# Triangular inverses one direction at a time, and 64-row products from compact operands

## The chip, the cores and the metric

The kernel runs on one core of a Trainium2 chip. The metric is the device time of one execution in microseconds (us). The engines are TensorE (PE; PEld is its loading of stationary operands), VectorE (DVE), ScalarE (ACT), GpSimd (POOL) and SyncE (SP), whose queue issues most of the DMAs.

## The reference, cut to what matters

Two residual blocks over 512 latent tokens (`S`) and 256 context tokens (`C`). The first has an attention layer and an "odd" layer with neighbourhood attention and a two-directional RWKV-7 scan; the second has a Mamba-2 scan and a gated delta rule (GDN), both in two directions, and a feed-forward network. RWKV and GDN run first over the context, and the state that comes out starts the run over the latent tokens. GDN in chunks of 64 tokens needs the solution of a unit triangular system per chunk, head and direction:

```python
a_mat = jnp.einsum("bclhd,bcshd->bclsh", k, k) * beta[:, :, :, None] * masked_exp(diff, strict)
lhs = jnp.moveaxis(a_mat, -1, 2) + jnp.eye(CHUNK, dtype=a_mat.dtype)
rhs = jnp.concatenate([v * beta[..., None], k * (beta * jnp.exp(g))[..., None]], -1)
sol = lax.linalg.triangular_solve(lhs, jnp.moveaxis(rhs, 3, 2), left_side=True, lower=True, unit_diagonal=True)
```

The RWKV recurrence `S = S*w - (S kk)(kk*a)^T + v k^T` is written in chunks in the same manner, so that it too needs the inverse of one unit triangular 64 x 64 matrix per chunk, head and direction. Products are float32; the large projections are split into a high and a low part (three products each).

## The kernel before, in words

All code is unrolled Python on a tile framework. The framework orders the instructions of each engine when the kernel is built: what is traced earlier has priority, and an instruction whose inputs are not ready lets later ones pass. After that the order is fixed. The program interleaves stages by generators: every `yield` gives the turn to the other generators, so the number of yields says how much of one stage is traced beside another. PSUM has 8 banks; pools take them by `bufs`, and a pool opened later waits for each bank until its last user is done.

The order around the change. `layer1` (L1331): **phase 1** of the RWKV context stream `c` (`rw_phase1`, L842), beside it `na_proj`; then phase 1 of the latent stream `l` with, as `self.side`, `rw_tri` and `rw_phase2` of the context stream (L1371 to L1374; one side step per iteration, two on odd iterations after the 16th); then `na_attn` (neighbourhood attention, L1205) with `rw_tri` of the latent stream stepped beside it (L1379 to L1382); then `rw_phase2` of the latent stream; then the output projection and the feed-forward network `f1`, whose side work is the whole context half of the second block, `ssm_ctx` (L2065), with its own triangular solve inside `ssm_tri`. `layer2` runs the latent half: `gdn_head`, then `ssm_tri` with `ssd_pair` ("pairs") and `gates` stepped beside it (L2157 to L2162), then the recurrence `gdn_rec` with `ssd_rec` and the output work.

`rw_dir` (L948) runs for each of 4 head pairs j and 2 directions d. It writes `az` (L983 to L989), a tile with zeros in one half of the partitions for each of the two heads, stores it (`dAf`, `dR`), multiplies it by `BKn` (L1004, 128 rows and both heads in one product), masks the result into `M` (L1006, DVE), multiplies `M` by `vu` (L1011), and copies (L1012, ACT). Groups of 2 chunks (latent) or 4 (context) share a PSUM bank.

`trisolve` (L769) inverts the 32 x 32 diagonal blocks of both directions by 31 steps of two DVE operations per direction: L792 multiplies into PSUM (`Tl`), L794 subtracts. The two directions alternate: multiply d0, multiply d1, subtract d0, subtract d1. There is a yield after every third step. Then ACT writes both transposes (L798) and the caller stores inverses and transposes of both directions (L1041: d0 on SP's queue, d1 on ACT's; L1735: all on SP's). There are four solves: RWKV context and latent, GDN context and latent. `rw_unit` (L1043) and `gdn_unit` (L1795) load them.

Of the kernel before, what the change touches and what calls it, by code (L numbers as in the profile page):

```python
# [766 lines left out]
class K1:  # L767

    def trisolve(self, pool, L, As, ps):  # L769


        nc = self.nc
        Zs, Ts = [], []
        for d in range(2):
            Z = pool.tile([128, 32, 32], F32, tag=f"Z{d}", name="Zl")
            nc.gpsimd.memset(Z, 0.0)
            nc.gpsimd.memset(Z.rearrange("p a b -> p (a b)")[:, ::33], 1.0)
            Zs.append(Z)
            Ts.append(ps[:, 256 * d:256 * d + 256])
        for n in range(1, 32):  # L780
            for op in range(2):
                for d in range(2):
                    A, Z = As[d], Zs[d]
                    if d == 0:
                        t = 32 - n
                        rows, cols, nr, ncl = slice(0, t), slice(t, 32), t, n
                    else:
                        t = n - 1
                        rows, cols, nr, ncl = slice(t + 1, 32), slice(0, t + 1), 31 - t, t + 1
                    tmp = Ts[d][:L, :nr * ncl].rearrange("p (a b) -> p a b", a=nr)  # L790
                    if op == 0:
                        nc.vector.tensor_tensor(tmp, A[:L, rows, t:t + 1].to_broadcast([L, nr, ncl]), Z[:L, t:t + 1, cols].to_broadcast([L, nr, ncl]), op=ALU.mult)  # L792
                    else:
                        nc.vector.tensor_tensor(Z[:L, rows, cols], Z[:L, rows, cols], tmp, op=ALU.subtract)  # L794
            if n % 3 == 0:
                yield
        for d in range(2):
            nc.scalar.activation(As[d][:L], Zs[d][:L].rearrange("p a b -> p b a"), AF.Copy)  # L798
        return Zs, As
# [42 lines left out]
    def rw_phase1(self, s):  # L842
# [4 lines left out]
        with ExitStack() as es:  # L847
# [7 lines left out]
            s.az = [pi.tile([128, s.nar, 2, n], F32, name=f"az{i}") for i in range(2)]  # L855
            s.vu = [pi.tile([128, s.nch, 128], F32, name=f"vu{i}") for i in range(2)]
            for z in s.az + s.vu:
                nc.gpsimd.memset(z, 0.0)
# [89 lines left out]
    def rw_dir(self, s, d, j, tp):  # L948
# [34 lines left out]
        for e in range(2):  # L983
            p = slice(64 * e, 64 * e + 64)
            if s.lat:
                nc.gpsimd.tensor_tensor(ch(az[p, 1, e]), ch(r[p]), E[p, :, i0:i0 + 64], op=ALU.mult)
                nc.sync.dma_start(s.dR[d][p, j], az[p, 1, e])
            nc.vector.tensor_tensor(ch(az[p, 0, e]), ch(kk[p]), E[p, :, iprev:iprev + 64], op=ALU.mult)
            nc.sync.dma_start(s.dAf[d][p, j], az[p, 0, e])  # L989
# [5 lines left out]
        w = nar * 128  # L995
        per = 512 // w
        mk = self.b(f"mar{d}")[:, :w].unsqueeze(1).to_broadcast([128, per, w])
        hc = max(per, nch // 2)
        for g in range(0, nch, per):
            if g % hc == 0:  # L1000
                M = tp.tile([128, hc, nar, 2, 64], F32, tag=f"M{d}", name="M", bufs=1)
            ps = s.psv("psA")
            for c in range(per):
                nc.tensor.matmul(ps[:, c * w:c * w + w], BKn[:, g + c].rearrange("p s t -> p (s t)"), az[:, :, :, (g + c) * 64:(g + c) * 64 + 64],  # L1004
                                 start=True, stop=True)
            nc.vector.tensor_tensor(M[:, g % hc:g % hc + per].rearrange("p c s e t -> p c (s e t)"), ps.rearrange("p (c x) -> p c x", c=per), mk, op=ALU.mult)  # L1006
            yield
            for c in range(g, g + per):
                for e in range(2):
                    o = ((c - g) // 2) * 128 + e * 64  # L1010
                    nc.tensor.matmul(ps[64 * (c % 2):64 * (c % 2) + 64, o:o + 64], M[:, c % hc, 0, e], vu[:, c, e * 64:e * 64 + 64], start=True, stop=True)  # L1011
            nc.scalar.activation(t2[:, g * 64:(g + per) * 64], ps[:, :per * 64], AF.Copy)  # L1012
            if (g + per) % hc == 0:
                g0 = g + per - hc
                for c in range(2):
                    nc.sync.dma_start(s.dA[d][:, c, g0 // 2:(g0 + hc) // 2, j].rearrange("p b e t -> p b (e t)"), M[0:64, c::2, 0].rearrange("p b e t -> p b (e t)"))
                if s.lat:
                    nc.sync.dma_start(s.dRR[d][:, j, g0:g0 + hc], M[:, :, 1].rearrange("p c e t -> p c (e t)"))
# [4 lines left out]
            yield  # L1023
        nc.sync.dma_start(s.dBV[d][:, j].rearrange("p b v -> p (b v)"), t2)

    def rw_tri(self, s):
        nc = self.nc
        Lq = 8 * s.nb
        with self.pool(name="tri", bufs=1, side="left") as trp, self.pool(name="trips", bufs=1, space=PSUM, side="right") as tps:
            As = [trp.tile([128, 32, 32], F32, tag=f"A{d}", name="Al") for d in range(2)]  # L1030
            for d in range(2):
                for p in range(4):
# [3 lines left out]
            Zs, ZTs = yield from self.trisolve(trp, 4 * Lq, As, tps.tile([128, 512], F32, name="Tl"))  # L1036
            for d in range(2):
                for z, dst in ((Zs[d], s.dZ[d]), (ZTs[d], s.dZT[d])):
# [364 lines left out]
class K2:  # L1403
# [308 lines left out]
    def ssm_tri(self, s):  # L1712
        nc = self.nc
        Lq = 8 * s.nb
        with self.pool(name="tri" + s.nm, bufs=1, side=s.side) as trp:
# [8 lines left out]
            else:  # L1724
                try:
                    while True:
                        next(tri)
# [384 lines left out]
    def layer2(self):  # L2112
# [20 lines left out]
        with ExitStack() as ps:  # L2133
# [23 lines left out]
            for _ in tri:  # L2157
                next(pairs, None)
                next(gates, None)
# [57 lines left out]
```

## Time and profile before

| | us |
|---|---|
| median of 3 runs | 3785.26 (3782.23 to 3792.06) |
| the profiled execution | 3793.68 |
| its span | 3791.9 |
| PE busy | 3377.0 |
| DVE busy | 1701.5 |

A row of a timeline has the start, the busy time, the engine, the line, the operation, the tiles (out<-in) and a count; in brackets stands how long the engine had been idle and what released it. A row by stretch has the length, the busy time of each engine with its number of instructions, the granted clock of PE (1.0 is 2.4 GHz, 0.5 is 1.2 GHz), and DMA. A row of waits has who waited for whom, us in total, times and the longest. The profiled execution is 0.2% above the median.

### The profile page before, as it was taken

To read this page: it belongs to the slowest core of one execution; us is meant where nothing else is said; L and a number is where in the kernel's file an instruction comes from. 1 tells how busy PE (TensorE), PEld (TensorE's weight loads), DVE (VectorE), ACT (ScalarE), POOL (GpSimd) and SP (SyncE) were. 2 spreads that over 40 slices of the span, in tenths; PEclk is the share of its full clock that TensorE was granted. 3 is DMA by queue.
4 is the path that set the end of the run, shared out by engine and by line. 5 is a ranking of instruction groups with operands and counts; after the bars stand their busy time and mean duration, and the time that the engine had idled before them with its cause. 6 is when DMAs were issued, how large, how long until landed. Compare 5 with 4: busy or idle time off the path is not lost. (4 is left out here: it accounts for less than half of the span.)

```text
span 3791.9 us, 49466 instructions
## 1 busy us (share of the span) xinstructions
PE 3377.0 (89%) x18772; PEld 2652.6 (70%) x18772; DVE 1701.5 (45%) x3170; ACT 1308.5 (35%) x2263; POOL 1402.0 (37%) x940
## 2 busy tenths in 40 slices
PE   7989989999999768888889989997898698789997
PEld 3679868787878546667768877666777457658885
DVE  4566231111124596574554426447657767431112
ACT  3366231121224433332234432333545323232222
POOL 1453222222223453321335544434544343244442
PEclk9999999999999878999889999998999899999999
DMA  6420243434334434636423433433455668512221
GB/s 230 164 106 7 88 151 117 150 116 141 126 106 129 111 111 140 175 88 204 146 70 124 131 105 95 122 93 99 140 155 155 158 193 247 164 61 95 95 97 65
DMA packets 397757, 480.78 MB, mean 127 GB/s; under 512 B 148432, under 2 KB 288656, under 8 KB 396496
## 3 DMA queue, kind: packets, MB, share of 16 engines
q1 hardware_dynamic: 384976, 476.05, 40.6%
q10 hardware_dynamic: 12544, 1.57, 0.3%
q8 instruction: 149, 2.44, 0.3%
q14 instruction: 88, 0.72, 0.1%
HBM read 391.86 MB, written 85.66 MB: 126 GB/s over the span
## 5 line engine op out<-in xcount | busy, mean ns | idle before, releaser
L322 POOL TENSOR_TENSOR wlo<-wraw,whi 128x1024 fp32r<-128x1024 f32 (+2 forms) x371 | 867.1, 2339 | 1512.7 <-ACT whi L321 1345.3
L321 ACT ACTIVATE whi<-wraw 128x1024 fp32r<-128x1024 f32 (+2 forms) x371 | 380.2, 1026 | 1041.3 <-issue 240.8
L504 DVE TENSOR_TENSOR pu<-pu,sg 128x512 f32<-128x512 f32 x88 | 55.6, 632 | 606.9 <-PE pu L361 554.2
L361 PE MATMUL pd<-hidh,wlo 128*128 128x512 f32 (+1 forms) x704 | 262.0, 372 | 9.2 <-POOL wlo L322 8.9
L361 PE MATMUL pd<-hidh,whi 128*128 128x512 f32 (+1 forms) x704 | 263.4, 374 | 6.1 <-ACT whi L321 3.8
L361 PE MATMUL pd<-hidl,whi 128*128 128x512 f32 (+1 forms) x704 | 260.5, 370 | 0.2 <-DVE hidl L506 0.2
L361 PE MATMUL pg<-hil,whi 128*128 128x512 f32 x528 | 214.3, 406 | 28.8 <-ACT hil L449 15.4
L361 PE MATMUL pg<-hil,wlo 128*128 128x512 f32 x528 | 211.4, 400 | 8.1 <-POOL wlo L322 7.1
L361 PE MATMUL pu<-hil,whi 128*128 128x512 f32 x528 | 209.7, 397 | 5.8 <-ACT whi L321 5.8
L361 PE MATMUL pu<-hil,wlo 128*128 128x512 f32 x528 | 209.2, 396 | 6.0 <-POOL wlo L322 6.0
L361 PE MATMUL pg<-lol,whi 128*128 128x512 f32 x528 | 210.5, 399 | 2.5 <-DVE lol L450 2.4
L361 PE MATMUL pu<-lol,whi 128*128 128x512 f32 x528 | 208.9, 396 | 0.0
L361 PE MATMUL psp<-hil,whi 128*128 128x512 f32 x416 | 174.0, 418 | 25.6 <-DVE yo L1782 11.8
L361 PE MATMUL psp<-lol,whi 128*128 128x512 f32 x416 | 171.0, 411 | 2.9 <-DVE lol L450 2.9
L361 PE MATMUL psp<-hil,wlo 128*128 128x512 f32 x416 | 170.3, 409 | 1.9 <-POOL wlo L322 1.8
L513 DVE SCALAR_TENSOR_TENSOR xT<-pd,mod,xT 128x512 f32<-128x512 f32 x80 | 59.8, 749 | 244.6 <-PE pd L361 244.6
L361 PEld LDWEIGHTS pd<-hidh,whi 128*128 128x128 f32 x704 | 133.3, 189 | 46.8 <-issue 15.1
L361 PEld LDWEIGHTS pd<-hidh,wlo 128*128 128x128 f32 x704 | 133.4, 189 | 39.1 <-POOL wlo L322 15.4
L361 PEld LDWEIGHTS pg<-hil,whi 128*128 128x128 f32 x528 | 101.5, 192 | 71.8 <-ACT hil L449 18.6
L361 PEld LDWEIGHTS pd<-hidl,whi 128*128 128x128 f32 x704 | 133.3, 189 | 24.0 <-issue 0.9
L792 DVE TENSOR_TENSOR Tl<-Al,Zl 64x31 f32<-64x31 f32 (+15 forms) x248 | 145.2, 585 | 4.1
L1574 DVE SCALAR_TENSOR_TENSOR psp<-xpl,vecs,psp 128x512 f32<-128x512 f32 x144 | 107.8, 751 | 84.5 <-ACT psp L1570 58.1
(588 smaller groups left out, 8145.9 us busy)
## 6 DMA issues: line engine op xcount, KB each, us to landing
mraw<-in_wm_dram SPq DMA_DIRECT2D x144, 512.0 KB, 4.3
wraw<-in_w2c_dram SPq DMA_DIRECT2D x72, 512.0 KB, 3.3
wraw<-in_wf0in_dram SPq DMA_DIRECT2D x44, 512.0 KB, 3.6
wraw<-in_wf1in_dram SPq DMA_DIRECT2D x44, 512.0 KB, 3.6
Z<-dZ SPq DMA_DIRECT2D x48, 256.0 KB, 3.8
ZT<-dZT SPq DMA_DIRECT2D x48, 256.0 KB, 4.1
wraw<-in_w1d_dram SPq DMA_DIRECT2D x23, 512.0 KB, 3.9
wraw<-in_wf2g_dram SPq DMA_DIRECT2D x22, 512.0 KB, 3.2
```

The costliest lines, as they stand in the source:

```text
L321: self.nc.scalar.activation(hi[:, :nk], t[:, :nk], AF.Copy)
L322: self.nc.gpsimd.tensor_tensor(lo[:, :nk], t[:, :nk], hi[:, :nk].bitcast(F32), op=ALU.subtract)
L361: nc.tensor.matmul(ps, l, r, start=first and i == 0 and p == 0, stop=last and i == n - 1 and p == 2)
L504: nc.vector.tensor_tensor(u, u, sg[:, :n], op=ALU.mult)
L513: nc.vector.scalar_tensor_tensor(x[:, j], pd[:, :n], gv[:, j:j + 1], x[:, j], op0=ALU.mult, op1=ALU.add)
L792: nc.vector.tensor_tensor(tmp, A[:L, rows, t:t + 1].to_broadcast([L, nr, ncl]), Z[:L, t:t + 1, cols].to_broadcast([L, nr, ncl]), op=ALU.mult)
L1574: nc.vector.scalar_tensor_tensor(pv, xp[:, :, t:t + L], w(t), pv, op0=ALU.mult, op1=ALU.add)
```

## The change

`trisolve` takes one direction: the 31 steps of d0 run to the end, each subtract directly behind its multiply, then ACT writes its transpose and the caller stores it; then d1. Yields come after every fifth step and, except in the context GDN, after each direction's stores (6 + 1 per direction); the context GDN solve, which had no yield inside, has 2 per direction. All stores go by SP's queue. The clearing of the `Z` tiles stands ahead of the loads. `az` has no zero halves any more: one operation and one store cover both heads, and the `az` tiles are no longer cleared. The products of L1004 become two per chunk, one per head, of 64 rows and half the columns, each head into a bank of its own; a group is 4 chunks in both streams, and `rw_dir` has 9 yields in the latent stream where it had 11. The latent phase 1 gets a third PSUM bank (`psd1f`), and the context phase 2 gives one up (`bc` 2 to 1). In `layer2` a turn of the solve steps `gates` or `pairs` by turns, where it stepped both.

```diff
-    def trisolve(self, pool, L, As, ps):
...
+    def trisolve(self, d, L, A, Z, T):
...
+        nc.gpsimd.memset(Z.rearrange("p a b -> p (a b)")[:, ::33], 1.0)
         for n in range(1, 32):
-            for op in range(2):
-                for d in range(2):
...
+            tmp = T[:L, :nr * ncl].rearrange("p (a b) -> p a b", a=nr)
+            nc.vector.tensor_tensor(tmp, A[:L, rows, t:t + 1].to_broadcast([L, nr, ncl]), Z[:L, t:t + 1, cols].to_broadcast([L, nr, ncl]), op=ALU.mult)
+            nc.vector.tensor_tensor(Z[:L, rows, cols], Z[:L, rows, cols], tmp, op=ALU.subtract)
+            if n % 5 == 0:
+                yield
+        nc.scalar.activation(A[:L], Z[:L].rearrange("p a b -> p b a"), AF.Copy)
...
-            s.az = [pi.tile([128, s.nar, 2, n], F32, name=f"az{i}") for i in range(2)]
+            s.az = [pi.tile([128, s.nar, n], F32, name=f"az{i}") for i in range(2)]
-            for z in s.az + s.vu:
+            for z in s.vu:
                 nc.gpsimd.memset(z, 0.0)
...
+        if s.lat:
+            nc.gpsimd.tensor_tensor(ch(az[:, 1]), ch(r), E[:, :, i0:i0 + 64], op=ALU.mult)
+            nc.sync.dma_start(s.dR[d][:, j], az[:, 1])
+        nc.vector.tensor_tensor(ch(az[:, 0]), ch(kk), E[:, :, iprev:iprev + 64], op=ALU.mult)
+        nc.sync.dma_start(s.dAf[d][:, j], az[:, 0])
...
+        w = nar * 64
+        per = 4
         for g in range(0, nch, per):
+            M = tp.tile([128, per, nar, 2, 64], F32, tag=f"M{d}", name="M", bufs=1)
+            pa = [s.psv("psA") for e in range(2)]
             for c in range(per):
+                for e in range(2):
+                    p = slice(64 * e, 64 * e + 64)
+                    nc.tensor.matmul(pa[e][:, c * w:c * w + w], BKn[p, g + c].rearrange("p s t -> p (s t)"), az[p, :, (g + c) * 64:(g + c) * 64 + 64],
+                                     start=True, stop=True)
+            for e in range(2):
+                nc.vector.tensor_tensor(M[:, :, :, e], pa[e][:, :per * w].rearrange("p (c s t) -> p c s t", c=per, t=64), mk, op=ALU.mult)
             yield
+            ps = pa[0]
...
             yield
+            if s.lat:
+                yield
...
     def rw_tri(self, s):
...
             for d in range(2):
-                for z, dst in ((Zs[d], s.dZ[d]), (ZTs[d], s.dZT[d])):
+                yield from self.trisolve(d, 4 * Lq, As[d], Zs[d], T[:, 256 * d:256 * d + 256])
+                for z, dst in ((Zs[d], s.dZ[d]), (As[d], s.dZT[d])):
                     for p in range(4):
                         sl = slice(32 * p, 32 * p + 32)
-                        (nc.sync, nc.scalar)[d].dma_start(dst[sl, :, sl].rearrange("i u j -> u i j"), z[Lq * p:Lq * p + Lq])
+                        nc.sync.dma_start(dst[sl, :, sl].rearrange("i u j -> u i j"), z[Lq * p:Lq * p + Lq])
+                yield
...
-            st_c.side, st_c.bq, st_c.bc, st_c.bl, st_c.bk = "right", 2, 2, 1, 1
+            st_c.side, st_c.bq, st_c.bc, st_c.bl, st_c.bk = "right", 2, 1, 1, 1
...
-        with self.pool(name="psd1c", bufs=2, space=PSUM) as pA, self.pool(name="psd1f", bufs=2, space=PSUM) as pD:
+        with self.pool(name="psd1c", bufs=2, space=PSUM) as pA, self.pool(name="psd1f", bufs=3, space=PSUM) as pD:
...
     def ssm_tri(self, s):
...
             for d in range(2):
-                for z, dst in ((Zs[d], s.dZ[d]), (ZTs[d], s.dZT[d])):
+                for i, _ in enumerate(self.trisolve(d, 4 * Lq, As[d], Zs[d], T[:, 256 * d:256 * d + 256])):
+                    if s.lat or i % 3 == 2:
+                        yield
+                for z, dst in ((Zs[d], s.dZ[d]), (As[d], s.dZT[d])):
...
+                if s.lat:
+                    yield
...
-            for _ in tri:
-                next(pairs, None)
-                next(gates, None)
+            for i, _ in enumerate(tri):
+                if i % 2:
+                    next(pairs, None)
+                else:
+                    next(gates, None)
```

## Rows read from the trace of the kernel before

**Rows 1.** The page, part 1: busy us, share of the span, instructions.

```profile
PE 3377.0 (89%) x18772; PEld 2652.6 (70%) x18772; DVE 1701.5 (45%) x3170; ACT 1308.5 (35%) x2263; POOL 1402.0 (37%) x940
```

**Rows 2.** Busy us of each engine by stretch, with PE's granted clock and DMA.

```profile
1330.00:1453.00 123.00, 85.35 (x403) 58.49 (x401) 110.42 (x192) 38.35 (x64) 53.11 (x31) 0.81 0.35 106
1453.00:1590.00 137.00, 110.15 (x696) 83.66 (x694) 82.63 (x135) 48.74 (x86) 48.64 (x43) 0.86 0.59 170
1605.00:1693.00 88.00, 84.07 (x547) 62.39 (x545) 72.44 (x221) 34.97 (x78) 26.29 (x30) 1.00 0.23 75
1693.00:1714.00 21.00, 2.77 (x21) 2.16 (x22) 0.86 (x2) 5.37 (x5) 1.68 (x3) 0.61 0.84 151
2306.00:2385.00 79.00, 73.02 (x301) 58.19 (x300) 66.95 (x139) 16.19 (x21) 28.84 (x14) 0.96 0.26 77
2886.00:2982.00 96.00, 79.04 (x379) 63.24 (x378) 91.92 (x171) 44.19 (x56) 42.01 (x22) 0.91 0.45 133
2982.00:3008.00 26.00, 8.42 (x45) 4.83 (x44) 10.54 (x18) 6.83 (x7) 5.30 (x3) 0.61 0.95 201
```

**Rows 3.** Timeline, all engines, where the latent phase 1 begins.

```profile
1295.30 3.55 POOL L858 MEMSET az<- 128x2048 f32 x2
...
1304.16 0.76 PE L361 MATMUL psz<-hil,whi 128*128 128x512 f32 x1 [12.12 <-DVE tw L871]
```

**Rows 4.** Groups of instructions by form, 1297 to 1590 us: count, busy us, mean ns.

```profile
L1004 PE MATMUL psA<-az,BKn 128*128 128x256 f32 x128 | 45.4, 482 | 40.2 <-DVE BKn L992 38.4 <-ACT t L1012 1.8
...
L986 POOL TENSOR_TENSOR az<-r,E 64x512 f32<-64x512 f32 x16 | 24.6, 1538 | 11.3 <-ACT E L976 10.5
...
L988 DVE TENSOR_TENSOR az<-kk,E 64x512 f32<-64x512 f32 x16 | 19.2, 1199 | 0.2
```

**Rows 5.** DVE's timeline in the latent phase 1, two stretches.

```profile
1323.13 0.42 DVE L927 TENSOR_SCALAR sqk<-sqk 128x512 f32<-128x512 f32 x1
1323.58 3.35 DVE L928 RECIPROCAL sqk<-sqk 128x512 f32<-128x512 f32 x1
...
1421.19 0.38 DVE L792 TENSOR_TENSOR Tl<-Al,Zl 64x220 f32<-64x220 f32 x1
1421.49 0.68 DVE L992 TENSOR_TENSOR BKn<-kd,t 128x512 f32<-128x512 f32 x1
1422.09 0.38 DVE L792 TENSOR_TENSOR Tl<-Al,Zl 64x220 f32<-64x220 f32 x1
1422.39 0.68 DVE L1006 TENSOR_TENSOR M<-psA,consts 128x512 f32<-128x512 f32 x1
1422.99 0.66 DVE L794 TENSOR_TENSOR Zl<-Zl,Tl 64x220 f32<-64x220 f32 x2
```

**Rows 6.** Groups by form, DVE, 2300 to 2390 us: one subtract by itself.

```profile
L794 DVE TENSOR_TENSOR Zl<-Zl,Tl 64x220 f32<-64x220 f32 x4 | 1.3, 370 | 0.0
```

**Rows 7.** Context phase 2 beside latent phase 1: one line's instructions, first and last start.

```profile
L1052 SPq DMA_DIRECT2D Z<-dZ x8: 319/344/545, 1465.5 to 1560.1; - x8
...
L1126 DVE TENSOR_TENSOR G<-G,psc x32: 269/286/292, 1490.5 to 1586.8; 64x128 f32<-64x128 f32 x32
```

**Rows 8.** Waits, 1297 to 1630 us.

```profile
PE psA L1004 <- DVE BKn L992: 38.4, 6, 11.1
...
ACT t L961 <- DMA dZT<-Al: 4.9, 1, 4.9
```

**Rows 9.** Waits, 1615 to 1860 us.

```profile
POOL U L1165 <- PE po L1289: 14.9, 1, 14.9
...
ACT ptile L1276 <- DMA dZT<-Al: 9.5, 1, 9.5
```

**Rows 10.** SP's queue behind the latent GDN solve.

```profile
2981.80 2.98 SPq L1735 DMA_DIRECT2D dZ<-Zl  x4
...
2992.42 3.74 SPq L1735 DMA_DIRECT2D dZT<-Al  x4
...
3000.40 0.32 SPq L1924 DMA_DIRECT2D xw<-ssl  x1
```

More of the change, by code (lines that the diff above doesn't have):

```diff
@@ L1010, in rw_dir @@
                     o = ((c - g) // 2) * 128 + e * 64
-                    nc.tensor.matmul(ps[64 * (c % 2):64 * (c % 2) + 64, o:o + 64], M[:, c % hc, 0, e], vu[:, c, e * 64:e * 64 + 64], start=True, stop=True)
+                    nc.tensor.matmul(ps[64 * (c % 2):64 * (c % 2) + 64, o:o + 64], M[:, c - g, 0, e], vu[:, c, e * 64:e * 64 + 64], start=True, stop=True)
             nc.scalar.activation(t2[:, g * 64:(g + per) * 64], ps[:, :per * 64], AF.Copy)
[L1013 to L1018, printed above, removed]
+            for c in range(2):
+                nc.sync.dma_start(s.dA[d][:, c, g // 2:(g + per) // 2, j].rearrange("p b e t -> p b (e t)"), M[0:64, c::2, 0].rearrange("p b e t -> p b (e t)"))
+            if s.lat:
+                nc.sync.dma_start(s.dRR[d][:, j, g:g + per], M[:, :, 1].rearrange("p c e t -> p c (e t)"))
             if g == 0:
@@ L1029, in rw_tri @@
         with self.pool(name="tri", bufs=1, side="left") as trp, self.pool(name="trips", bufs=1, space=PSUM, side="right") as tps:
-            As = [trp.tile([128, 32, 32], F32, tag=f"A{d}", name="Al") for d in range(2)]
+            T = tps.tile([128, 512], F32, name="Tl")
+            As, Zs = ([trp.tile([128, 32, 32], F32, tag=f"{n}{d}", name=f"{n}l") for d in range(2)] for n in "AZ")
             for d in range(2):
+                nc.gpsimd.memset(Zs[d], 0.0)
                 for p in range(4):
@@ L1715, in ssm_tri @@
         with self.pool(name="tri" + s.nm, bufs=1, side=s.side) as trp:
-            As = [trp.tile([128, 32, 32], F32, tag=f"A{d}", name="Al") for d in range(2)]
+            As, Zs = ([trp.tile([128, 32, 32], F32, tag=f"{n}{d}", name=f"{n}l") for d in range(2)] for n in "AZ")
             for d in range(2):
+                nc.gpsimd.memset(Zs[d], 0.0)
                 for q in range(4):
@@ L1720, in ssm_tri @@
                     nc.sync.dma_start(As[d][Lq * q:Lq * q + Lq], s.dA[32 * q:32 * q + 32, d, :, c0:c0 + 32].rearrange("i u j -> u i j"))
-            tri = self.trisolve(trp, 4 * Lq, As, s.psd("Tl"))
-            if s.lat:
-                Zs, ZTs = yield from tri
[L1724 to L1727, printed above, removed]
-                except StopIteration as e:
-                    Zs, ZTs = e.value
-                yield
+            T = s.psd("Tl")
             for d in range(2):
-                for z, dst in ((Zs[d], s.dZ[d]), (ZTs[d], s.dZT[d])):
+                for i, _ in enumerate(self.trisolve(d, 4 * Lq, As[d], Zs[d], T[:, 256 * d:256 * d + 256])):
+                    if s.lat or i % 3 == 2:
+                        yield
+                for z, dst in ((Zs[d], s.dZ[d]), (As[d], s.dZT[d])):
                     for q in range(4):
```

49 lines of the change are left out of this document (8 added, 41 removed).

## The prediction

> **What bounds the kernel now.** I read the page's busy times first, then the busy time by stretch around each of the four triangular solves, and there the timelines and the waits. Over the whole span PE is busy 3377 of 3792 us [rows 1], so most of the kernel is PE work that the change doesn't touch. The change lies in three places, and the reader should see in [rows 2] that these are where PE is not the bound:
>
> - A, latent RWKV phase 1 with the context solve and the context phase 2 beside it (1297 to 1590). From 1330 to 1453 DVE is busy 110 of 123 us and PE 85, at a granted clock of 0.81, a mixture of both levels. PE's longest wait is for DVE's `BKn`, 38.4 us [rows 8].
> - B, the latent RWKV solve beside neighbourhood attention. Until 1693 PE is full (84 of 88); then come 21 us in which PE works 2.8: a dead stretch of 18 us between the solve's end and the latent phase 2.
> - D, the latent GDN solve beside pairs and gates. DVE is full (92 of 96); then 26 us with 8.4 us of PE: a second dead stretch of 18 us before the recurrence.
>
> The context GDN solve (C, 2306 to 2385) lies beside a feed-forward network that keeps PE busy 73 of 79 us [rows 2]; there is little to win there.
>
> **Serial solves.** The instruction count stays: 62 multiplies and 62 subtracts per solve. Two subtracts of different directions overlap today: a pair takes 0.66 us [rows 5] and one alone 0.37 [rows 6], so 0.08 us is saved per pair. An instruction that reads what the one before it wrote starts 0.03 us after that one's end (0.42 us at 1323.13, next start 1323.58) [rows 5]. In the new order no pair is left: 31 pairs x (0.08 + 0.03) = 3.4 us more DVE time per solve, 14 us for four. Multiplies of one step are not back to back today (another instruction stands between them in [rows 5]), so they lose nothing. Below nothing it can't be, since no instruction goes away; upper bound: all 124 boundaries lose 0.11, 13.6 us per solve. I take 3.4, because the pairs of [rows 5] show just these overlaps. It costs time in D, where DVE is full (+3.4), and in A (+3.4); in B and C PE is the engine that is full, and it hides there (if that cover is gone, 3.4 each).
>
> The VectorE: DVE Perf Modes page of the Trainium skill, section "The DRAIN you can't avoid", says that a read behind a write on the same engine needs a semaphore, but that chained copies with a semaphore after each took as long as without. By that the serial order would cost nothing beyond the 3.4 us; the 0.03 us of rows 5 agrees with it.
>
> **Order on DVE.** In A the scheduler puts a phase 1 instruction wherever the next solve instruction isn't ready: multiply, other, multiply, other, two subtracts, other [rows 5]. That is 3 others per step of both directions. With one direction at a time each of 4 boundaries is open, so 4 others. Phase 1 gets DVE sooner, the solve later. If others are always waiting, this is 31 more of them ahead of the solve's end at about 0.7 us (L992 and L1006 in [rows 5]): up to 21 us later. The total of DVE isn't changed by this.
>
> **Compact operands.** L988 goes from 16 instructions to 8 of the same length per lane: 19.2 / 2 = 9.6 us less DVE; L986 likewise, 12.3 us less POOL [rows 4]. Half of the DVE gain falls in the stretch where DVE is full: 4.8 us, of which the serial solve takes 3.4 back; the rest lies beside PE work. So about -1.5, and I add -1.5 for L986, whose removal frees the readers of `az`. The `az` clearing (3.55 us on POOL) stands ahead of the addition that DVE and, through it, PE wait for (12.1 us idle) [rows 3]: -3.5, on the path. 24 fewer SP issues lie beside other work: nothing.
>
> **64-row products.** L1004 streams 64 products of 256 columns now, 128 of 128 then: the same columns. No 64-row product is in the trace, so bounds: if two heads run at once, half of the 45 us of records [rows 4], up to -23; if a record of half the columns took as long as a whole one does now (0.48 us), twice as many would be 45 us more. In between lies equal streaming, 0, which I take, since a product of half the columns has half to stream; and PE isn't full in A [rows 2]. DVE's masks keep their number in the latent stream.
>
> TensorEngine Tiling (Array Packing) of the Trainium skill, section "Key Properties", says that row tiles work independently but that a change of the tiling mode drains the engine; "Theoretical Speedup" gives up to 2x for a contraction of at most 64. By the second, L1004 would fall to some 23 us; the first speaks against it, since a group now changes shape at each border. No row of before shows either, and both ends lie inside the bounds above.
>
> **Stores.** All stores go to SP. In A, ACT's `t` waited 4.9 us behind its own queue's stores [rows 8]: -3, since PE's psa product waited for it. In B the same queue held up `ptile` for 9.5 us; `ptile` is what the last attention product waits for, and POOL's clearing of `U` waits 14.9 us for that product [rows 9], because phase 2's memory is the attention's. With ACT free and d0 stored in the middle of the attention, what is late next is d1: its 8 stores on SP and its loads, still some 7 us. So of 18 us dead, -11; bounds: -18 (all) and 0 (d1's end is as late as now and the d0 work can't begin). Behind d1's stores on SP stand the first loads of phase 2, 10 us today as well.
>
> In D the 16 stores fill SP from 2981.8 to 2996.2 (the last group starts 2992.42 and takes 3.74); the scan's first load `xw` waits behind them until 3000.4 [rows 10]. In the new order d0's 8 stores are out long before, and d1's come with 6 rounds of pairs still to do (18 rounds; 5 before the solve, 7 beside it, against 10 today). So most of the 18 us dead can fill up, but the pairs' tail, now without the solve's cover, and the +3.4 eat part: -8 net; bounds -18 and +8 (the tail of two pairs exposed).
>
> **Yields and the context phase 2.** Counted from the code: the latent phase 1 has 4 + 4 x 12 = 52 iterations and gives 52 + 18 = 70 side steps; the side needs 10 (solve) + 64 (8 units of 8 rounds) = 74. After: 4 + 4 x 10 = 44 iterations, 58 steps, and the side needs 14 + 64 = 78. So 20 rounds, 2.5 units, instead of 4 rounds are traced behind phase 1. The units take (1586.8 - 1465.5) / 8 = 15 us each, beside phase 1 [rows 7]; the lower bound is 0, since the scheduler goes by readiness and priority only breaks ties, and phase 1 then competes for a shorter time. The upper bound is 2.5 x 15 = 37, all of them exposed. I take +3, near the lower end, because the starts of the eight units reach over 95 us of phase 1 [rows 7].
>
> **C.** Solve steps spread over 4 turns instead of 1, d0's stores earlier, three turns more for the side work, and the network has enough turns left to hide them (54 against 46): 0, bounds -5 and +6 (the 6 us that PE lacks in the stretch [rows 2], either way).
>
> **Sum.** A: -3.5 - 1.5 - 1.5 - 3 + 3 = -6.5; B -11; C 0; D -8: -25.5 us. The profiled execution took 3793.68 us, 1.8 more than its span, and is 0.2% over the median of 3785.3; -25.5 gives 3768 for such an execution and 3760 against the median.
>
> **Rivals.** (1) The dead stretches stay: d1's chain takes the place of both directions' chain, because the serial solve ends later on a full DVE. For it: DVE full in D and the open boundaries of [rows 5]; against: d0 is stored early, and in B DVE is busy only 72 of 88. Then B and D give nothing and A -6.5: 3779; with D's +3.4 and more, up to 3785. (2) Slower: the context phase 2 comes late. Its units are a chain; the attention's score banks in PSUM are its banks, so attention can't begin before its last unit. The solve ends up to 21 us later and 2.5 units stand behind phase 1. It decides the sign from the point at which this delay is over 25 us; at 21 + 2.5 x 10 = 45 us and with A's other gains, B and D as forecast, 3760 + 42 = 3802. For it: its last update today, at 1586.8, is just at the end of stage A [rows 7], with only 4 rounds behind phase 1; against: the scheduler does place its units early. (3) Row pairs run at once and both dead stretches vanish: -23 x 0.4 = -9 (taking 0.4 as the part of A that PE sets) and 14 more from the 17 us that the forecast leaves dead in B and D: 3737. (4) The change doesn't serialise what it says (the scheduler lets d1 run beside d0, since nothing but priority keeps them apart): then only the stores and `az` count, about 3770, inside the forecast.
>
> **How the numbers follow.** Forecast (with 4): 0.50, own range 3742 to 3773. Rival 1: 0.22. Rival 2: 0.18, of which some 0.02 comes out as no change. Rival 3: 0.10. A measurement of this kernel can tell about 0.3% (11 us) from no change: 3774 and 3797 are the borders. Faster: 0.50 + 0.10 = 0.60; same: 0.22 + 0.02 = 0.24; slower: 0.16. The range leaves out the far half of rivals 2 and 3: 3732 to 3800.
>
> **What would show it.** `az` clearing gone and PE's 12 us gap at the phase's start down to about 8.5. L792 and L794 by turns with one other between them in A. PE's dead stretches behind the solves of B and D down to about 7 and 10 us. Context phase 2's last `G` update against the first score product of the attention: if these move apart from phase 1's end by more than 25 us, rival 2 is true. L1004 starts at the same time for both heads if rows run together. The prediction is wrong above all if A's order changes more than its sums.

## The result and the profile after

The changed kernel takes 3830.17 us (median; 3825.56 to 3836.44) against 3784.03 us for the kernel before: 1.2% slower, ratio 1.0119, 95% interval 1.0097 to 1.0141. Its profiled execution took 3836.44 us (before: 3793.68), its span is 3834.5.

Where the time went is read by stages. The table gives by how much each stage of a profiled execution is longer (+) or shorter (-) than that of before, in us. A+B runs from the latent phase 1's first product to the first product of f1 (666.2 us before), C from there to the first product of `layer2`'s latent half (642.6), D from there to the first product of the latent recurrence (434.2). "attention" is the start of the attention's scores, counted from the start of A, "phase 1" the end of phase 1's last product of `az` and `BKn`. The stages are single executions: the changed kernel profiled twice (the last two lines) differs by up to 4 us in A+B, C and D and by 8 in the other two columns, and e2 below, which has the same code up to the end of C, has A+B at +4.4. Shifts of a few us therefore say nothing by themselves.

| kernel | phase 1 | attention | A+B | C | D |
|---|---|---|---|---|---|
| RWKV part alone (e4) | -29.5 | -12.0 | -14.4 | +0.2 | +2.0 |
| solve part alone (e5) | +28.3 | +37.3 | +26.6 | +7.9 | +22.3 |
| after, first profile | -4.5 | +20.0 | +9.8 | +3.8 | +25.0 |
| after, again (e12) | +3.2 | +27.8 | +13.8 | +7.1 | +23.7 |

So D lost most, A+B second, C a little, if anything; and the two halves of the change work against each other.

The busy times by stretch of the changed kernel (columns: stretch, length, busy us of PE, PEld, DVE, ACT, POOL, then granted clock, DMA share, GB/s), to be laid beside [rows 2]:

```profile
1313.00:1443.00 130.00, 89.97 (x452) 67.46 (x452) 110.76 (x194) 45.63 (x64) 61.42 (x34) 0.82 0.35 103
1696.00:1725.00 29.00, 20.45 (x160) 15.44 (x159) 10.26 (x29) 12.11 (x24) 7.32 (x12) 0.96 0.32 84
2320.00:2386.00 66.00, 49.73 (x201) 39.35 (x199) 56.43 (x132) 12.56 (x15) 17.41 (x9) 0.86 0.26 62
2905.00:2976.00 71.00, 47.97 (x230) 38.14 (x228) 66.15 (x144) 21.40 (x27) 17.81 (x9) 0.85 0.41 111
2976.00:3040.00 64.00, 40.80 (x198) 31.03 (x198) 24.62 (x33) 23.20 (x31) 23.05 (x14) 0.74 0.47 126
```

The reader is to see three things. The dead stretch of B has filled up: 20 of 29 us are PE work where it was 2.8 of 21. In C, PE works 50 of 66 us, where [rows 2] have 73 of 79. In D the solve is done in 70 us instead of 95, but 64 us of pairs follow it, in which no engine is full: DVE, which was the full one, works 25 of 64.

The waits of the changed kernel, from 2300 to 2400 and from 2905 to 3052 us (columns: who waited for whom, us in total, times, longest):

```profile
ACT Al L786 <- DVE Zl L783: 21.8, 2, 19.1
PE pd L361 <- ACT whi L321: 14.0, 1, 14.0
...
PE py L1766 <- DVE W L1752: 19.5, 2, 11.7
PE psp L361 <- ACT whi L321: 12.1, 1, 12.1
```

`Al L786` is the transposed copy that follows each direction. In the kernel before, the copy's longest wait in the first of these stretches was 6.2 us:

```profile
ACT Al L798 <- DVE Zl L794: 6.2, 1, 6.2
```

In the changed kernel the second copy of C waits 19.1 us for the solve, and the weights' rounding `whi` stands behind it in ACT's order, though SP had issued its last load of weights by 2365.5:

```profile
2386.50 1.93 ACT L786 ACTIVATE Al<-Zl 64x1024 f32<-64x1024 f32 x1 [19.06 <-DVE Zl L783]
2388.34 1.56 ACT L321 ACTIVATE whi<-wraw 128x768 fp32r<-128x768 f32 x2
```

PE's wait of 14.0 us for `whi` ends only then. SP's queue does the same in A. From 1297 to 1610 us its longest single waits include one that the kernel before doesn't have:

```profile
SPq L1046 <- POOL U L1155: 22.2, 1, 22.2
```

### The profile page after: what moved, and what is told of

Read it like the earlier page. It is cut to its first block, busy times and chain, and to the rows that moved or that the text cites. A ratio compares the mean times of both kernels' runs of the same rounds, so it can differ in the third digit from the quotient of the medians.

```text
span 3834.5 us, 49733 instructions
## 1 busy us (share of the span) xinstructions
PE 3403.5 (89%) x18964; PEld 2680.6 (70%) x18964; DVE 1685.4 (44%) x3162; ACT 1302.1 (34%) x2243; POOL 1384.2 (36%) x928
## 5 line engine op out<-in xcount | busy, mean ns | idle before, releaser
L361 PE MATMUL psp<-hil,whi 128*128 128x512 f32 x416 | 175.8, 423 | 35.8 <-ACT whi L321 12.1
L361 PEld LDWEIGHTS pd<-hidh,whi 128*128 128x128 f32 x704 | 133.8, 190 | 58.5 <-ACT whi L321 21.3
L782 DVE TENSOR_TENSOR Tl<-Al,Zl 64x60 f32<-64x60 f32 (+23 forms) x248 | 131.9, 532 | 7.8 <-DMA Al<-ssc 1.9
```

What stands on the lines that cost most here:

```text
L361: nc.tensor.matmul(ps, l, r, start=first and i == 0 and p == 0, stop=last and i == n - 1 and p == 2)
```

## The experiments

They ran in five groups, each on a chip of its own with the kernel before beside it: e1 and e3 to e5; e2 and e6 to e8; e9 to e12; e13 to e16; e17 and e18. The kernel before takes 3797.9 to 3799.4 us (medians) there, and each ratio is against it in the same group. The kernel before has only the one profile, of the first measurement, and all stage shifts are against that one: behind D, where no kernel differs, the experiments lie -0.6 to +8.9 us from it.

**The two halves (e4, e5).** e4 takes the solves, their stores and the turns of layer 2 from before and keeps the RWKV part (compact operands, 64-row products, PSUM banks); e5 is the reverse.

> The RWKV part alone: compact operands, 64-row products, one and three PSUM buffers as in the changed kernel; the four solves, their stores and the alternation of pairs and gates as before. Theory S (the 46 us that the change costs come from the solves' form: ACT's queue held up by a transposed copy in C and D, and a tail of pairs in D; the RWKV part is about neutral): stages C and D go back to before, some 30 us of the 46 come back, leaving the context stream's lost 6 to 10 us in phase 1 and a later attention: 3790 to 3803. Rival R (the RWKV part pays most, since everything from the context phase 1 on starts later): over 3815.

> The kernel before with the serial solves, their stores on SP and the alternation of pairs and gates alone; operands, products and PSUM as before. Theory S: C loses 6 us and D some 24, B gains at most 11: 3800 to 3820. Rival R: only the RWKV part costs time, this one is within 11 us of before, 3775 to 3795.

Measured: e4 0.9956 (0.9939 to 0.9973), e5 1.0143 (1.0123 to 1.0162). The halves add up to the whole: -0.44 + 1.43 = +0.99%, and the changed kernel in its group is at 1.0097 (1.0064 to 1.0129; e12, expected as follows). Rival R fell: the RWKV part gains. Theory S named the right half but missed both prices: it held the RWKV part for about neutral, and 1.43% is 54 us, half of it in A+B.

> The changed kernel once more, unaltered, on the chip of the experiments: what the others are to be compared with. By the first comparison 1.0% to 1.4% above before.

**Three cures (e1, e2, e3, e6).**

```diff
-        nc.scalar.activation(A[:L], Z[:L].rearrange("p a b -> p b a"), AF.Copy)    # e1, e6
+        nc.vector.tensor_copy(A[:L], Z[:L].rearrange("p a b -> p b a"))
-                if i % 2: next(pairs, None)    # e2, e6
-                else: next(gates, None)
+                next(pairs, None)
+                next(gates, None)
-                self.step(2 if i > 16 and i % 2 else 1)    # e3, e6
+                self.step(2 if i > 8 else 1)
```

> The changed kernel with the transposed copy behind each direction on VectorE instead of ScalarE (four copies, one line). Theory Q (ACT's queue stands behind this copy, which waits up to 19 us for the solve; the feed-forward network's and the pairs' ACT work stands behind it, and PE behind that): PE's waits of 14.0 us in C and 12.1 us in D for ACT go away, the time falls by 10 to 25 us, to 3805 to 3820. Rival (the copy only shows where the network was waiting anyway, and the four copies cost VectorE as much where it is full): within 6 us of the changed kernel's 3830.

> The changed kernel with one edit undone: beside the latent GDN solve each turn steps a pair and a gate again, not one of them by turns. Theory T (stage D's 24 us come mostly from the turns: with 6 rounds of pairs beside the solve instead of 10, the rest stands behind the solve, where PE waits for VectorE's `W` 11.7 and 7.8 us): the last py product comes 10 to 20 us sooner after the solve's end, the time falls by that, to 0.65% to 0.95% above the kernel before (the changed kernel is 1.2% above). Rival U (the tail is there because the solve keeps VectorE to itself, whichever order the turns have): within 5 us of the changed kernel, 1.05% to 1.3% above.

> The changed kernel with two side steps per iteration of the latent phase 1 from iteration 9 on (79 steps instead of 58, so that the context phase 2's 78 all lie beside phase 1). Theory P (the context phase 2 ends 25 us later because 20 of its rounds stand behind phase 1 in the program's order): its last update of G falls back to within 5 us of phase 1's end, the attention starts some 20 us sooner and the end gains the 8 us that A and B lose: 3815 to 3825. Rival (the order of the program is only a preference, and the units are late because their inputs and engines are): G's last update stays 30 us or more behind phase 1's end, time within 5 us of 3830.

> The changed kernel with three edits together: the transposed copy on VectorE, both pair and gate at each turn, and two side steps per iteration of the latent phase 1 from iteration 9 on. Theory V (these three are the whole loss: ACT's queue in C and D, the turns in D, the late context phase 2 in A): 1.2% above before falls by 0.3 (copy) + 0.3 to 0.5 (turns) + 0.3 (steps) to between 0.1% above and 0.2% below the kernel before. Rival W (the serial order itself costs in A and D, since the solve has VectorE to itself and what stands beside it waits): 0.4% to 0.8% above before.

| kernel | ratio (95%) | attention | A+B | C | D |
|---|---|---|---|---|---|
| e1 | 1.0067 (1.0048 to 1.0085) | +18.2 | +2.0 | +0.2 | +14.8 |
| e2 | 1.0064 (1.0049 to 1.0079) | +17.9 | +4.4 | +3.8 | +11.1 |
| e3 | 1.0086 (1.0070 to 1.0102) | +0.5 | -1.7 | +8.1 | +23.6 |
| e6 | 1.0042 (1.0027 to 1.0057) | 0.0 | -4.4 | +5.5 | +6.5 |

D's 25 us are in good part the turns (14 back with e2) and the copy on ACT (10 back with e1); the two overlap, for together (e6) 18 come back, and 6.5 stay. e3 puts the attention's start back to its old time, so theory P's mechanism is right for the 20 us there. Its price isn't: 1.0086 against e12's 1.0097 is within the two intervals, where P had 5 to 15 us; a late attention is partly caught up in B. Against the first measurement of the changed kernel (1.0119) e1 and e2 are clear gains, against e12 the intervals overlap; e2 ends just below T's range. e6 lies in W's range, at its lower end, so three cures don't bring the kernel back. But W's reason doesn't hold: the serial order by itself costs 0.27% (e13 below). What the cures leave is in the solve part all the same: e9 below, with the same RWKV part and side steps and the old solves, is 1.0% lower than e6.

Theory Q is right in D, where PE's wait of 12.1 us for `whi` falls to 1.6 in e1, and not in C. There e1's waits from 2300 to 2400 us read:

```profile
ACT whi L321 <- DMA wraw<-in_wf1out_dram: 23.2, 2, 23.0
...
PE pd L361 <- ACT whi L321: 16.2, 1, 16.2
```

and SP's queue in the same place (start, duration, line, transfer):

```profile
2349.83 1.26 SPq L1720 DMA_DIRECT2D dZT<-Al  x2
2351.20 4.49 SPq L315 DMA_DIRECT2D wraw<-in_wf1out_dram  x2
2380.29 2.20 SPq L1720 DMA_DIRECT2D dZ<-Zl  x4
```

PE's wait is still there (16.2 us, 14.0 in the changed kernel): with ACT free, `whi` now waits for its weights, and their load stands on SP behind the store of direction 1, which waits from 2355.7 to 2380.3 for the solve. The copy and the store block two queues at once, and freeing one left the wait as long as it was.

**What of the solve part it is (e13, e17, e18).** e13 changes the kernel before only in the order: the loop over directions stands outside the 31 steps. e17 adds the placing of the change (copy and stores right behind each direction, all stores on SP, the clearing of `Z` ahead of the loads). e18 adds instead four pulls per RWKV solve (a pull is one turn of the side work, up to its next yield).

```diff
-        for n in range(1, 32):
-            for op in range(2):
-                for d in range(2):
+        for d in range(2):
+            for n in range(1, 32):
+                    ...
+                    if n % 6 == 0: yield    # e18: n % 5, and one behind each direction's stores
```

> The kernel before with one edit: within each of the four solves direction 0 is solved to its end, then direction 1. Number of yields, copies, stores, their queues and everything else as before. The step of the prediction (one more phase 1 instruction gets in per solve step, so the solve ends up to 21 us later and phase 1 sooner; 3.4 us more VectorE time): solve later, phase 1's end sooner or equal, time within 0.2% of before. Theory S3 (the other way: the solve's instructions follow each other on VectorE and fewer others get in between; the solve ends sooner, the work beside it is late): the first solve ends 10 to 30 us sooner, phase 1's end 10 to 30 us later, fewer than 101 and 63 others within the first and the last solve, time 0.5% to 1.1% above before.

> e13 (the kernel before with each solve's directions one after the other, 0.27% above before) and, beside it, the placing of the change: direction 0's transposed copy on ScalarE and its stores stand right behind direction 0, all stores on SP. Pulls (10 per solve) and turns as before. Theory H (SP's and ScalarE's queues stand behind a store and a copy that wait for the solve, and what feeds phase 1 and the pairs stands behind them): phase 1 ends 15 to 30 us later than in e13, D loses 8 to 12, 0.8% to 1.3% above before. Rival I (the queues bear it, the pulls and the turns are what e5 loses beyond e13): within 0.15% of e13, 0.15% to 0.45% above before.

> e13 with four pulls more in the RWKV solves: 12 within the solve and one behind each direction's stores, 14 instead of 10. Copies, stores and turns as in e13. By theory H this costs little beyond e13: 0.2% to 0.5% above before. By rival I the context phase 2's loads and clearings, that come four pulls later in the program's order, stand behind phase 1's on SP and POOL (in e5 SP waits 32 us for one of them): phase 1 ends 15 to 30 us later than in e13, 0.6% to 1.1% above before.

Measured: e13 1.0027 (1.0015 to 1.0038), e17 1.0139 (1.0117 to 1.0160), e18 1.0046 (1.0032 to 1.0061). The placing costs 1.1% of the 1.43% that e5 loses, the serial order 0.3%; the 0.2% of the pulls lies within the two intervals. Rival I fell, in e17 as in e18. Theory H holds, with phase 1 even later than it said: 37 us behind e13's. e13 itself lies between its two expectations: the first solve ends sooner, as S3 had it, but phase 1 ends no later (+0.2 us). Stage shifts of e17: A+B +31.3, C +8.6, D +8.5; of e13: -0.5, +6.4, +0.1. D's +22.3 in e5 against +8.5 here are the turns again. The terms don't add up exactly (e5 is not slower than e17 by what turns and pulls cost apart); which of them cover each other was not followed further.

Why, the queues show. First e13's POOL and SP behind the context solve, then e17's:

```profile
1427.74 0.99 POOL L1162 MEMSET U<- 128x512 f32 x2
1427.27 0.43 SPq L1050 DMA_DIRECT2D ZT<-dZT  x1
1428.30 0.79 SPq L1053 DMA_DIRECT2D U<-rwc  x2
1431.41 0.55 SPq L986 DMA_DIRECT2D rwl<-az  x1
```

```profile
1418.09 2.19 SPq L1030 DMA_DIRECT2D dZ<-Zl  x4
1427.04 0.44 SPq L1042 DMA_DIRECT2D ZT<-dZT  x1
1458.17 1.04 POOL L856 TENSOR_TENSOR ms<-zp 128x512 f32<-128x512 f32 x1 [16.32 <-ACT zp L854]
1459.15 0.98 POOL L1154 MEMSET U<- 128x512 f32 x2
1459.70 0.79 SPq L1045 DMA_DIRECT2D U<-rwc  x2
1462.77 1.28 SPq L976 DMA_DIRECT2D rwl<-az  x1
```

In e13 `U` is cleared at 1427.74 and SP goes on at once. In e17 the clearing stands in POOL's order behind `ms`, which waits 16.3 us for ACT's `zp`; SP stands at the load into `U` for 32 us (1427.5 to 1459.7), and phase 1's own stores (`az`, 1462.77) and loads stand behind it. Ahead of that SP had waited 21.3 us for direction 1 at the store `dZ<-Zl` of 1418.09. In this stretch the DMA engines run nearly dry, first e13, then e17:

```profile
1420.00:1470.00 50.00, 30.46 (x191) 24.63 (x192) 35.19 (x44) 15.42 (x26) 20.84 (x16) 0.73 0.51 138
```

```profile
1420.00:1470.00 50.00, 28.04 (x118) 19.77 (x118) 28.43 (x27) 12.58 (x20) 19.99 (x13) 0.69 0.20 44
```

44 GB/s instead of 138. The third pair of `BKn` follows at 1524 and 1531 us in e17, at 1497 and 1504 in e13: the 27 us are there. That the clearing of `U` comes late because its memory is that of the solve's tiles, which the stores must have left, is inferred from the order of these rows, not tried.

**The term on yields, alone (e15), and with the RWKV part (e9, e10).** e15 is the kernel before with fewer side steps (`2 if i > 40 and i % 2 else 1`, 58); e9 and e10 are e4 and e7 with more (`2 if i > 8 else 1`).

> The kernel before with 58 side steps beside the latent phase 1 instead of 70, as many as the changed kernel has. The term on yields, alone: 16 of 74 rounds are left behind phase 1. The prediction took 3 us of it, bound 37. Theory P: the context phase 2's last update comes 10 to 20 us later, the attention too, part is won back there: time 0.1% to 0.4% above before. Rival: order of the program is only a preference, within 0.1% of before.

> The RWKV part alone (e4) with two side steps per iteration of the latent phase 1 from iteration 9 on. In e4 phase 1 ends at 1548.5 but the context phase 2's last update of G comes at 1579.5, 31 us behind. Theory P2 (the same lateness as in the changed kernel, hidden by the sooner phase 1): G's last update moves to within 10 us of phase 1's end, the attention starts 10 to 18 us sooner, the time is 0.7% to 0.9% below before (e4: 0.44%). Rival (phase 1 then gets later by as much, since VectorE is full in this stretch): within 0.1% of e4.

> As e9, with all the RWKV solves' stores on SP (e7 with the two side steps). If the stores' queue matters behind the latent solve once attention starts sooner: 0.1% to 0.2% below e9; if not: within 0.1% of e9.

Measured: e15 1.0026 (1.0015 to 1.0037), attention +13.5, A+B +9.8. e9 0.9944 (0.9928 to 0.9961), attention -29.2, A+B -26.7. e10 0.9961 (0.9946 to 0.9975). Theory P's mechanism holds twice: with 12 steps fewer the attention is 13.5 us late, and more steps bring e4's attention 17 us forward. At the end the missing steps cost 0.26%, as P said, while e4's gain of 0.1% by more steps lies within the two intervals: there P2 (0.7% to 0.9% below before) was wrong about the price. e10 isn't faster than e9 either. e9, the RWKV part with the old solves and more side steps, has the lowest ratio of this study, 0.56% below before; e4, e10 and e14 lie within its interval.

**Stores on SP with the paired solves (e7).**

```diff
-                        (nc.sync, nc.scalar)[d].dma_start(dst[sl, :, sl].rearrange("i u j -> u i j"), z[Lq * p:Lq * p + Lq])
+                        nc.sync.dma_start(dst[sl, :, sl].rearrange("i u j -> u i j"), z[Lq * p:Lq * p + Lq])
```

> The RWKV part alone, as in e4, with the stores of both directions of the RWKV solves on SP instead of half of them on ScalarE. The prediction's steps for A and B: with ScalarE's queue free, `t` isn't late (3 us in A), and the gap of 12 us before the attention's last products goes, 6 to 11 us in B: the time is 0.65% to 0.8% below before (e4 was 0.44% below). Rival (the gap is set by the solve's end, 16 stores on SP end no sooner and the first loads of the latent phase 2 stand behind them): within 0.1% of e4 or slower, 0.3% to 0.5% below before.

Measured 0.9973 (0.9962 to 0.9985): no better than e4, as the rival had it. From the attention's start to phase 2 it is 8.4 us shorter than before, e4 2.7, but phase 1 ends 5 us later than e4's. What B gains, A gives away.

**What of the RWKV part it is (e8, e11, e16, e14).** e8 gives the kernel before the new PSUM banks. e11 splits e4's multiplies into `az` by halves of the partitions again, e16 is e11 with more side steps. Both split DVE's and POOL's multiply. e14 exchanges the two loops around e4's 64-row products.

```diff
-            nc.gpsimd.tensor_tensor(ch(az[:, 1]), ch(r), E[:, :, i0:i0 + 64], op=ALU.mult)    # e11, e16
-        nc.vector.tensor_tensor(ch(az[:, 0]), ch(kk), E[:, :, iprev:iprev + 64], op=ALU.mult)
+        for e in range(2):
+            p = slice(64 * e, 64 * e + 64)
+            ... nc.gpsimd.tensor_tensor(ch(az[p, 1]), ch(r[p]), E[p, :, i0:i0 + 64], op=ALU.mult)
+            nc.vector.tensor_tensor(ch(az[p, 0]), ch(kk[p]), E[p, :, iprev:iprev + 64], op=ALU.mult)
-            for c in range(per):    # e14
-                for e in range(2):
+            for e in range(2):
+                for c in range(per):
```

> The kernel before with the PSUM banks alone as in the changed kernel: three buffers instead of two for the latent phase 1's direction work, one instead of two for the context phase 2. The RWKV part as a whole makes phase 1 end 25 us sooner and the kernel 0.44% faster. If the third buffer is the cause: phase 1 ends 15 to 25 us sooner here too, 0.2% to 0.4% below before. If it is the operands and the 64-row products: phase 1 within 5 us of before, time within 0.1%, or slower by up to 0.2% since the context phase 2 has one buffer less.

> The RWKV part alone (e4) with each multiply into `az` split in two of 64 partitions again, on VectorE and on POOL; the operands stay compact and the products of 64 rows. Theory O (phase 1 ends 25 us sooner in e4 because VectorE, full in this stretch, has 8 instructions of 1.2 us less): phase 1's end goes back by 8 to 15 us, time 0.1% to 0.3% below before. Rival N (it is TensorE: products of two heads that run at once): phase 1 within 5 us of e4's, time within 0.1% of e4's.

> e11 (compact operands, 64-row products, the multiplies into `az` in halves) with two side steps per iteration from iteration 9 on: what is left against the kernel before is the products of 64 rows and the banks. If the products cost nothing, as the prediction took it, e11's 0.63% above before was the late context phase 2 and this one is within 0.2% of before. If they cost phase 1 its 12 us: 0.2% to 0.5% above before.

> The RWKV part alone (e4) with the 64-row products of head 0 issued first and those of head 1 after them, instead of by turns. If products of different row halves run at once only where they stand next to each other in TensorE's order: in e4 114 of 274 records have a partner within 0.05 us, here below 30, their busy time goes from 42.6 to 48 or more us. Time: TensorE isn't what phase 1 waits for, within 0.2% of e4 (0.44% below before); if it is, 0.1% above to 0.2% below before.

Measured: e8 1.0005 (0.9995 to 1.0016), so it isn't the banks. e11 1.0063 (1.0037 to 1.0089), phase 1 33 us later than in e4: the two multiplies in halves cost 1.07%, beyond what theory O expected. With enough side steps (e16 1.0001, 0.9989 to 1.0013, against e9's 0.9944) it is 0.57%, 22 us. e16 is level with before, so what else the RWKV part brings (64-row products, banks, single stores, no clearing of `az`, with steps that make up for its fewer yields) is worth nothing together. DVE's groups from 1200 to 1600 us, e4 and then e11 (count, busy us, mean ns):

```profile
L986 DVE TENSOR_TENSOR az<-kk,E 128x512 f32<-128x512 f32 x8 | 7.6, 945 | 0.0
L986 DVE TENSOR_TENSOR az<-kk,E 128x256 f32<-128x256 f32 x6 | 2.5, 413 | 0.0
```

```profile
L987 DVE TENSOR_TENSOR az<-kk,E 64x512 f32<-64x512 f32 x16 | 19.5, 1216 | 0.2
L987 DVE TENSOR_TENSOR az<-kk,E 64x256 f32<-64x256 f32 x12 | 8.9, 741 | 0.1
```

That is 12 us of DVE in the latent stream and 6 in the context stream. POOL's share falls from 24.0 to 16.8 us in the same stretch; which of the two engines' halves costs the time was not tried apart. PE's waits for `BKn`, which stands behind `az` on DVE, fall too, from e11 to e4:

```profile
PE psA L1005 <- DVE BKn L993: 60.3, 9, 13.8
```

```profile
PE psA L1002 <- DVE BKn L990: 38.3, 6, 11.2
```

These waits don't tell the whole: the kernel before, with halves, has 38.4 us [rows 8], as much as e4, and its phase 1 ends 29.5 us later.

e14 0.9957 (0.9940 to 0.9974), the same as e4: the order of the products costs nothing. In the trace it goes the way that was expected, though less far: the records with a partner within 0.05 us fall from 128 of 288 to 70 (below 30 expected), their busy time rises from 42.6 to 46.8 us (48 or more expected). One group of 16 at the same place, e4 and then e14:

```profile
1409.85 2.08 PE L1002 MATMUL psA<-az,BKn 64*128 64x128 f32 x16 [11.16 <-DVE BKn L990]
```

```profile
1409.41 3.06 PE L1002 MATMUL psA<-az,BKn 64*128 64x128 f32 x16 [11.17 <-DVE BKn L990]
```

Both stand behind a wait of 11.2 us for DVE: a microsecond of PE here is not on the path.

## Why the prediction was wrong

Forecast -25.5 us, measured +46, outside the range and on the other side of no change. Step by step:

- **Stores, and where they stand (-22 forecast: -3 in A, -11 in B, -8 in D).** This is the step that failed. It priced how long SP and ACT are busy with stores, and counted the wait of a load behind them. It did not ask what stands behind the first store on its queue while that store itself waits for the solve. The stores and the copy come early in the queues, and the queues stand: ACT 19.1 us in C and SP 22.2 us in A in the changed kernel, SP 21.3 and 32.2 us in A in e17. e17 against e13 puts 1.1%, some 42 us, on this placing. Which of the waiting stores, loads and copies costs how much was not tried apart. In B the forecast seems to come about: the dead stretch is filled, and from the attention's start to phase 2 the changed kernel takes 14 us less. But e7, with the stores off ACT's queue, gains nothing at the end, and the 14 us go with the attention's late start: with the attention on time (e3) the stretch from its start to phase 2 is 1.6 us shorter than before, PE busy 100.6 of 120.0 us there against 99.4 of 121.6:

```profile
1594.90:1714.90 120.00, 100.58 (x643) 76.29 (x642) 82.01 (x236) 45.90 (x92) 30.52 (x38) 0.95 0.48 108
```

```profile
1592.30:1713.90 121.60, 99.36 (x640) 74.54 (x639) 77.78 (x236) 45.89 (x92) 30.97 (x37) 0.93 0.41 101
```

- **D (-8, upper bound +8).** Measured +24 to +25. "The pairs' tail, now without the solve's cover" was named and priced at 8 at most. The tail is 64 us from the solve's end to the last `py` product, where it was 14. Undoing the turns gives 14 of the 25 us back (e2), the copy off ACT 10 (e1), both together 18 (e6). So the bound on the pairs' tail was the second thing that failed.
- **Order on DVE.** Wrong in direction. It took every boundary between solve instructions as open to others. But a subtract is ready 0.03 us after its multiply, so a solve by one direction runs on:

```profile
1400.54 0.42 DVE L790 TENSOR_TENSOR Tl<-Al,Zl 64x252 f32<-64x252 f32 x1
1400.99 0.41 DVE L791 TENSOR_TENSOR Zl<-Zl,Tl 64x252 f32<-64x252 f32 x1
1401.43 0.42 DVE L790 TENSOR_TENSOR Tl<-Al,Zl 64x255 f32<-64x255 f32 x1
```

  (e13.) In [rows 5] another stands behind each multiply. Within the first solve 54 other instructions run on DVE in e13 instead of 85, within the last 38 instead of 46 (the 101 and 63 of e13's expectation count DVE's semaphore waits too), and the first solve ends 34 us sooner, not up to 21 later. For the end this is worth little (e13: 0.27%).
- **Serial solves (+3.4 us of DVE each).** About right where POOL stretches as many multiplies as before (11 and 11 in A, 3 and 2 in B): in e13 DVE's solve time in A goes from 53.5 to 55.8 us, in B from 45.0 to 46.9. In C and D it falls, 58.5 to 53.1 and 60.2 to 55.1, which the prediction had ruled out ("Below nothing it can't be"); see the last section.
- **Yields (+3, bound 37).** Right mechanism, mis-sized: 0.26% (10 us) in e15, 13.5 us at the attention's start. Rival 2 described it: the last `G` update comes 37 us behind phase 1's end (1611.7 against 1574.7), where it came 13 us behind it (1586.8 [rows 7] against 1573.8); by the prediction's own sign, a move of more than 25 us, that is 24, just short. But its price was overrated as a cause of the loss: with the lateness cured (e3) the kernel is still 0.86% slower.
- **Compact operands (-3 on the path).** Right in kind, far too small: 22 us (e16 against e9) to 41 us (e11 against e4). The step halved the DVE time saved and let the serial solve eat it. PE's waits for `BKn` in [rows 8] could have warned that DVE's time ahead of `BKn` is PE's, but that it is DVE's multiply and not POOL's is argued, not shown.
- **`az` clearing (-3.5).** Right about the wait: PE's wait at the start of the phase goes from 12.1 us [rows 3] to 6.6. What it is worth at the end was not tried alone.
- **64-row products (0, bounds -23 and +45).** Right at the end (e14, e16). In the trace the lower bound is real in part, since two heads do run at once where they stand side by side; the upper one isn't, for even issued head by head the latent products are busy 41.5 us (e14) against 45.4 [rows 4]. The page "TensorEngine Tiling (Array Packing)" of the Trainium skill, section "Theoretical Speedup", would have it up to twice as fast. e4's rows agree for the groups that pair up (2.08 against 3.06 us), but only 128 of 288 records do.
- **C (0, bounds -5 and +6).** Measured +4 to +7, of which some 4 are within what single profiles differ by. The prediction looked at the network's number of turns, not at its weights, which share SP and ACT with the solve.

Rivals 1 and 3 didn't come about; rival 4 is excluded, since in the trace after all 31 steps of one direction run before the first of the other, in all four solves. What the prediction lacked is a rival in which a moved store or copy blocks its queue.

## What to carry to other kernels

Before moving a store or a copy ahead in the program, list what comes behind it on the same queue, and take the time that it waits there as theirs: an engine's idle queue is free only for instructions that are ready. When two parts of a change touch one stretch, price the operations that the bottleneck's next step waits for at their full time: multiplies in halves ahead of `BKn` and its products cost more (22 to 41 us) than all the rest of the RWKV part, and the forecast had 3. And a solve that ends sooner need not help: e13's first solve ends 34 us sooner, phase 1 beside it ends when it did, and the kernel is 0.27% slower.

## What the runs showed of the hardware

**Multiplies stretched by POOL.** The solve's multiply, with both operands in SBUF, takes 0.38 us in the median and up to 2.6 at most. In the kernel before 40 of 248 multiplies take over 0.8 us, 71 us together; in all 40 POOL is running, for 90% of their time on average (11% in the other 208). None of the 248 subtracts, which read one operand from PSUM, takes over 0.42. In e13, with POOL's row below DVE's:

```profile
1395.08 0.39 DVE L791 TENSOR_TENSOR Zl<-Zl,Tl 64x231 f32<-64x231 f32 x1
1395.50 2.37 DVE L790 TENSOR_TENSOR Tl<-Al,Zl 64x240 f32<-64x240 f32 x1
1397.91 0.40 DVE L791 TENSOR_TENSOR Zl<-Zl,Tl 64x240 f32<-64x240 f32 x1
...
1395.22 2.38 POOL L322 TENSOR_TENSOR wlo<-wraw,whi 128x1024 fp32r<-128x1024 f32 x1 [5.49 <-PE psz L361]
```

The multiply ends 0.3 us after POOL does. The page "SBUF — State Buffer" of the Trainium skill, section "SBUF: two separate sides", states this as a rule: a VectorE operation with two SBUF inputs and a GpSimd operation that reads SBUF exclude each other for a whole instruction. The trace agrees. It is also where the serial solve saves DVE time in C and D: 8 stretched multiplies in each in e13, 14 us together, where 13 were, 24 to 25 us.

**Row pairs.** Products of 64 rows of the two heads run at once where they are issued by turns: 128 of 288 records start 4 to 40 ns from a partner (e4). 16 records of one group then take 2.08 us, issued head by head 3.06 (e4 and e14 above).
